# A depthwise convolution beside attention: its columns divided between GpSimd and VectorE, or all on GpSimd

## The chip, the core and the metric

The kernel runs on one NeuronCore of a Trainium2 chip. A core has five engines that run side by side, each working through its own queue in order: TensorE (PE: matrix products; its weight loads are listed as PEld), VectorE (DVE), ScalarE (ACT), GpSimd (POOL) and SyncE (SP, which here only starts transfers). They read and write a common on-chip memory of 128 partitions, and wait for one another at semaphores. The metric is the device time of one execution in microseconds (us); lower is better.

## What is computed

Two layers of a transformer over 1024 latent tokens with a prefix of 256 context tokens, width 1024, all in float32. Each layer normalises and modulates the tokens, projects them to parallel head groups, and adds a mixture of experts behind them. The head groups are attention with 8 query heads and 2 key and value heads of 64 columns, a pooling mixer, and a convolution module, whose 31 taps are the subject here. Cut to what matters:

```python
ql = apply_rope(rms_heads(heads(ql, N_Q_HEADS), q_gain[l]), cos, sin)
attn_l = latent_attention(ql, k_all, v_all)      # softmax over all 1280 keys
yl = jnp.concatenate([attn_l, pool_mixer(ul, ...), conv_module(al, gl, ...)], axis=-1) @ w_out[l]
...
def conv_module(a, g, w_dw, b_dw, cv_g, cv_b, w_pw):
    u = a * jax.nn.sigmoid(g)
    y = lax.conv_general_dilated(u, w_dw[:, None, :], window_strides=(1,),
                                 padding=[(CONV_K // 2, CONV_K // 2)],
                                 dimension_numbers=('NWC', 'WIO', 'NWC'),
                                 feature_group_count=CONV_W) + b_dw
    return jax.nn.silu(ln_affine(y, cv_g, cv_b)) @ w_pw
```

The convolution is depthwise: each of 256 channels has its own 31 weights along the tokens. The first layer computes context and latent tokens, the second only the latent ones (its context tokens give keys and values alone).

## The kernel before

A layer goes through these stages one after the other: a first pass (norms, pooling and convolution inputs), a second pass (queries, keys, values), attention with the convolution beside it, the output projection with routing, and the experts.

**The convolution's data.** Tile A holds the convolution's input with channels on the partitions, 128 channels in each of two halves (f = 0, 1), tokens along the columns; Y receives the result. With the padding between and beside the segments LC is 1340 columns in the first layer and 1054 in the second, so n = LC - 30 is 1310 and 1024 columns of output. A tap (f, k) multiplies a shifted view of A with the channel's weight and adds it to Y; there are 2 x 31 = 62 taps in a layer.

**The division.** CVM = 54 (line 49) says how many of 64 parts of the columns belong to GpSimd: m = 1105 of 1310, and 864 of 1024. `conv_setup` (line 1199) makes two lists. `convq` holds GpSimd's 62 taps; each is two instructions, a product into a scratch region (line 1222) and an addition to Y (line 1223), except the first of each half, which is one (line 1220). `convr` holds VectorE's 62 taps over the other 205 or 160 columns; each is a single instruction (line 1232, the first of each half line 1230) that reads A and Y and writes Y.

**Attention.** `attention` (line 1241) describes its work to a small list scheduler, the class Plan: each operation has an engine, a planned length, what it depends on, and a rank with a name, from which and from the table ATT an order of issue for each engine is fixed when the program is built. The hardware then follows these orders. Pairs of query tiles are taken in turn: in the first layer one short pair (the context's queries, 256 keys), then four full pairs (1280 keys); in the second layer the four full pairs. A pair has 16 steps (8 heads, 2 tiles). A step is: products of queries and keys (PE, lines 1337 and 1338), row maximum (DVE, line 1343, for 1024 and 256 columns apart), its negation (DVE, line 1347), exponential (ACT, line 1355), transposes of the result (PE, line 1360), their copies out of PSUM (DVE line 1367 or ACT line 1369), and products with the values (PE, line 1404). Queries are prepared by lines 1297 to 1313, and each pair's outputs are divided by the sums of the exponentials at lines 1428 to 1446.

**Where the convolution stands in it.** After the queries of the last tile (the list `tail`), the whole of `convq` is one operation of GpSimd (line 1275). Each of `convr`'s taps is an operation of VectorE with the planned length 0.07 + 1.33 * (1 - CVM / 64) = 0.28 us, ranked 3.5 us apart (lines 1276 and 1277). At the end of the plan stand the first steps of the convolution's norm and product (`cpost_steps`): PE transposes two tiles of Y (line 1499). They depend on all of the convolution. Behind attention, `outproj` reads its result (first product at line 1613).

Of the kernel before, what the change touches and what calls it, by code (L numbers as in the profile page):

```python
# [33 lines left out]
# ring of the experts' weights: units of 8 KB per partition, six to an expert; some of them open before the others  # L34
NU, NU0 = 14, 10
# ring of split slices, slices split ahead
# [3 lines left out]
def f32(ap):  # L40
# [7 lines left out]
# of 64 parts of the convolution's columns, those of GpSimd  # L48
CVM = 54
# the attention: microseconds by which operations may come later than their place in the order of the heads  # L50
ATT = {
# [7 lines left out]
class Plan:  # L59
    """operations of several engines with their lengths in microseconds, issued in the order of a list schedule"""  # L60
    LAG = {"DMA": 1.0}

    def __init__(self, prio=None, **slots):
        """slots: numbers of buffers that are taken in turn. prio: by name, the microseconds by which an operation may come later"""
        self.ops, self.slots, self.givers, self.prio = [], slots, {}, prio or {}

    def add(self, eng, length, f, deps=(), rank=(0.0, ""), at=0.0, take=None, give=(), after=None):
        """f issues the operation; eng may be several engines, length and f then lists. A buffer that an operation takes is free
        again after the operations that give it back. rank: microseconds by which it may come later, and its name. after: an
        operation of the same engine that is issued before"""  # L70
        e = [eng] if isinstance(eng, str) else list(eng)
        n = [length] if isinstance(eng, str) else list(length)
        fs = [f] if isinstance(eng, str) else list(f)
        k = len(self.ops)
        self.ops.append((list(zip(e, n, fs)), sorted({d for d in deps if d is not None}), rank, at, take, after))
        for g in give:
            self.givers.setdefault(g, []).append(k)
        return k

    def run(self):  # L80
        """of what can start first, the operation with the longest way to the end goes first"""
# [49 lines left out]
def weave(main, fill):  # L131
    """emit the steps of main in order, those of fill spread among them"""
    j, n, m = 0, len(main), len(fill)
    for i, s in enumerate(main):
        s()
        while j * n < (i + 1) * m:
            fill[j]()
            j += 1
    while j < m:
        fill[j]()  # L140
        j += 1


class Kernel:
# [6 lines left out]
    def later(self, f):  # L151
        """put off a store, so that loads behind it in the queue don't wait for its data"""
        self.stores.append(f)
# [29 lines left out]
    def ln_start(self, src, n=D):  # L183
        """mean and 1 / sqrt(variance + EPS) over n columns"""
# [73 lines left out]
    def mod_load(self, n, pool=None):  # L258
        """start the loads of up to the n-th next step"""
# [9 lines left out]
    def mod_step(self, ahead=1, pool=None):  # L269
# [15 lines left out]
        if k == KD - 1:  # L285
# [5 lines left out]
            if g == 0:  # L291
                # columns to partitions: shift and 1 + scale
# [9 lines left out]
    def layer(self, l):  # L302
# [11 lines left out]
        # blocks of 256 tokens in the order of the passes; the last two of the first pass start the second  # L314
# [42 lines left out]
    # weights of a pass: four units of two k-slices, split in two parts each  # L357
# [36 lines left out]
    def comb_open(self, ctx, l, ny, nx, side="left"):  # L394
        """the tiles that are loaded ahead lie where the last weights but one were; returns a pool that is put below them"""
# [12 lines left out]
    def behind(self, load, i):  # L408
        """a load that lets the scatter of one of the last three experts go first"""
# [17 lines left out]
    def comb0(self, i, t, eng):  # L427
        """gated sum of a token's two experts, times the modulation's gate"""
        self.comb0a(i, t)
        self.comb0b(i, t, eng)  # L430
# [13 lines left out]
    def comb_diag(self, tile_, i):  # L444
        """the gates of a tile's tokens on diagonals"""
# [5 lines left out]
    def comb_pe(self, t, g, ps):  # L451
        """the gated sum by products with diagonals, times the modulation's gate"""
# [12 lines left out]
    def comb2s(self, t):  # L465
        """norm by the vector engine alone, in two steps"""
# [23 lines left out]
    def pass1(self):  # L490
        nc, a, l, last = self.nc, self.a, self.l, self.last
        v, pool = nc.vector, nc.gpsimd
        with ExitStack() as ctx:
# [66 lines left out]
            def th(b):  # L560
                """a block to columns, modulated and split"""
# [138 lines left out]
    def plan1(self, order, sp, below, raws, Wh, Wl, PS, load, where, pb):  # L700
        """first pass of a later layer: combination of the experts' outputs, second residual, norms, products"""
# [18 lines left out]
        # weights of this pass  # L720
# [230 lines left out]
        for n in range(1, nb):  # L951
# [8 lines left out]
            # weights of the second pass  # L960
# [8 lines left out]
    def pass2(self, sp):  # L969
# [3 lines left out]
        with ExitStack() as ctx:  # L973
# [41 lines left out]
            def post(t, part, src=None):  # L1015
                """heads' norms and positions of the queries (part 0), the keys (part 1) or both (part 2), in stages"""
# [183 lines left out]
    def conv_setup(self):  # L1200
# [11 lines left out]
        m = n * CVM // 64  # L1212

        def tap(f, k):
            """the first columns"""
            y, x = self.Y[:, f, 15:15 + m], self.A[:, f, k:k + m]
            t = (self.Y[:, 1, 15:15 + m] if f == 0 else self.A[:, 0, 0:m])
# [7 lines left out]
        def rest(f, k):  # L1225
            """the other columns"""
            y, x = self.Y[:, f, 15 + m:15 + n], self.A[:, f, k + m:k + n]
            w = wdw[:, f, k:k + 1]
            if k == 0:
                nc.vector.tensor_scalar(y, x, w, small[:, 0, f:f + 1], op0=OP.mult, op1=OP.add)  # L1230
            else:
                nc.vector.scalar_tensor_tensor(y, x, w, y, op0=OP.mult, op1=OP.add)  # L1232
        self.convr = [lambda f=f, k=k: rest(f, k) for f in range(2) for k in range(CONV_K)]
# [6 lines left out]
    def attention(self, tail):  # L1240
        nc, l, last = self.nc, self.l, self.last
        with ExitStack() as ctx:
# [19 lines left out]
            def parts(pi):  # L1262
                """columns of the scores: up to 1024 and the rest"""
                n = pairs[pi][1] * 128
                return [(0, min(1024, n))] + ([(1024, n - 1024)] if n > 1024 else [])
# [4 lines left out]
            # the queries of the last tile, then the convolution  # L1270
# [4 lines left out]
            conv = [add(POOL, 4.33 * CONV_K * 2 * CVM / 64, lambda: [c() for c in self.convq], [lastq], (-1000.0, "conv"))]  # L1275
            for k, f in enumerate(self.convr):
                x = add(DVE, 0.07 + 1.33 * (1 - CVM / 64), f, [x], (3.5 * k, "cv"))
            conv.append(x)
# [138 lines left out]
            def norm(pi):  # L1417
                """divide the heads' outputs by the sums of the exponentials"""
# [47 lines left out]
            # the first tiles of the convolution's result  # L1466
# [16 lines left out]
    def cpost_steps(self, sp, pp, q, nm="cps"):  # L1483
        """for a pair of token tiles"""
# [55 lines left out]
    def outproj(self):  # L1540
# [3 lines left out]
        with ExitStack() as ctx:  # L1544
# [61 lines left out]
            def plain(k):  # L1606
                """a slice of the first tile's product, before the weights are split"""
# [53 lines left out]
            def last_res(hf):  # L1661
                """the last tile: first residual and its sums by halves of the columns"""
# [140 lines left out]
    def route_setup(self, wp):  # L1803
# [14 lines left out]
        # per expert: its number + 32 * (assignments in earlier tiles)  # L1818
# [11 lines left out]
    def route(self, ps, t0, t1):  # L1830
        """groups, experts and ranks of the tokens of some tiles; stops after each step"""
# [97 lines left out]
    def pump(self, n=1):  # L1929
        """the next steps of the routing, between other work"""  # L1930
# [9 lines left out]
    def scatters(self, n):  # L1940
        """write the numbers of some assignments to their places"""
# [47 lines left out]
    def route_rows(self, sp):  # L1989
        """where the halves of the products' rows go, counted in half rows: one of the first four chunks of at most 64 tokens  # L1990
        has the second halves of its rows 64 partitions further on"""
# [20 lines left out]
    def moe_open(self):  # L2012
        """buffers for the experts' weights, first loads"""
# [8 lines left out]
    def unit(self, e, j):  # L2022
        """two slices of an expert's weights: four units of gate and up, two of down"""
# [3 lines left out]
    def e_loads(self, lim, q=None):  # L2027
        """start the loads that find room: up to a number of units"""
# [15 lines left out]
    def moe(self):  # L2044
# [3 lines left out]
        with ExitStack() as ctx:  # L2048
# [45 lines left out]
            def prep(e):  # L2094
                """split the tokens and the first slices"""
# [5 lines left out]
            def half(ps, e):  # L2101
                """at most 64 tokens: the two halves of the columns go to two column tiles of the array,
                rows 64 to 127 of the products are the second half"""
# [21 lines left out]
            def full(ps, e, x=None):  # L2125
                """the first half of the columns is ready before the second; then the tokens of a second chunk"""
# [10 lines left out]
            def double(ps, p2, e, m):  # L2137
                """two chunks of tokens; the last place of the slices holds the second one's parts"""
# [45 lines left out]
            def scatter(y, idx, free=True):  # L2184
                """halves of rows to their places"""
# [14 lines left out]
            def one(e, x, ps, g, idx, free, n, lim):  # L2200
                """a whole chunk"""
# [12 lines left out]
            def more(e, n, j, ps, g):  # L2214
                """chunks from the third on"""
# [277 lines left out]
```

## Time and profile before

| | |
|---|---|
| time, median of 3 runs | 3312.55 us (3311.83 to 3315.14) |
| span of the profiled execution, first to last instruction | 3305.2 us |
| its own device time beside the span | not listed apart; the three runs lie 6.6 to 9.9 us above the span |
| PE busy | 2668.3 us (81%) |
| PEld busy | 1678.9 us (51%) |
| DVE busy | 1650.0 us (50%) |
| ACT busy | 1187.4 us (36%) |
| POOL busy | 1006.7 us (30%) |
| mean granted clock of TensorE | 0.906 of full speed |

Busy shares over the whole span mix stages with different limits. The span is better read in slices: the page cuts it into 40 equal ones of 82.6 us and gives each engine's busy share in tenths, and the clock that TensorE was granted in tenths of full speed. Attention fills about 305 to 698 us in the first layer and 1960 to 2307 us in the second.

### The profile page before, as it was taken

What the parts mean: (1) busy time and instruction counts of PE and PEld (TensorE: products, weight loads), DVE (VectorE), ACT (ScalarE), POOL (GpSimd) and SP (SyncE); (2) the same over time, 40 slices, a digit from 0 to 9 for tenths busy, and PEclk for the clock granted to TensorE, in tenths of its full rate; (3) what the DMA queues carried; (4) which work ended last, traced back from release to release, by engine and by line L of the source; (5) the groups of instructions that cost most, each with busy time, mean ns of one, the idle gap of its engine ahead of it and who ended that gap; (6) DMA issues with size and microseconds to landing.
All of it is one profiled execution on the core that took longest, in us unless ns stands there. A gap on an engine that the chain in (4) does not pass through costs nothing. (4 is left out here: it accounts for less than half of the span.)

```text
span 3305.2 us, 41725 instructions
## 1 busy us (share of the span) xinstructions
PE 2668.3 (81%) x13118; PEld 1678.9 (51%) x13118; DVE 1650.0 (50%) x2980; ACT 1187.4 (36%) x2255; POOL 1006.7 (30%) x919
## 2 busy tenths in 40 slices
PE   6987589998678878879756986999967788798884
PEld 4765356667445345446226764565753345454431
DVE  3356975568744323334139669555871233333215
ACT  3223356652134223324125434666311233333212
POOL 1024995013321211211126349900232111111114
PEclk8988789999889989999988998999988899898997
DMA  8541000032487875765986530000359986655895
GB/s 274 202 137 68 1 1 1 1 102 105 182 313 285 302 265 200 258 248 213 365 314 205 170 140 1 1 1 5 143 184 354 348 310 239 228 194 183 318 376 226
DMA packets 280607, 616.66 MB, mean 187 GB/s; under 512 B 63376, under 2 KB 77072, under 8 KB 271504
## 3 DMA queue, kind: packets, MB, share of 16 engines
q1 hardware_dynamic: 251696, 562.24, 46.6%
q0 software_dynamic: 24544, 37.91, 3.3%
q10 hardware_dynamic: 3712, 8.88, 0.7%
q8 instruction: 276, 4.52, 0.6%
q14 instruction: 379, 3.10, 0.3%
HBM read 577.09 MB, written 73.81 MB: 197 GB/s over the span
## 5 line engine op out<-in xcount | busy, mean ns | idle before, releaser
L1343 DVE TENSOR_REDUCE mx<-S 128x1 f32<-128x1024 f32 (+1 forms) x272 | 214.9, 795 | 163.1 <-PE S L1338 163.0
L174 PE MATMUL gu<-wh,xh 128*128 128x512 f32 x432 | 189.8, 439 | 117.2 <-issue 88.4
L1360 PE MATMUL pt<-ident,P 128*128 128x128 f32 x1312 | 221.1, 295 | 78.3 <-ACT P L1355 72.2
L1355 ACT ACTIVATE P<-S,nb 128x256 f32<-128x256 f32 (+1 forms) x272 | 208.6, 773 | 129.5 <-DVE nb L1347 128.1
L2174 PE MATMUL mpy<-er,g 128*128 128x512 f32 (+1 forms) x672 | 243.4, 633 | 8.3 <-issue 8.0
L180 POOL TENSOR_TENSOR rs_out<-ln_ve,mhalf 128x1 f32<-128x1 f32 x64 | 58.7, 918 | 606.2 <-DVE ln_ve L199 372.1
L2188 POOL DMA_INDIRECT y_d<-my,pl x128 | 139.3, 1088 | 315.5 <-ACTq L2280 107.6
L1360 PEld LDWEIGHTS pt<-ident,P 128*128 128x128 f32 x1312 | 152.9, 148 | 158.5 <-ACT P L1355 106.3
L2157 DVE TENSOR_TENSOR sg<-gu,sg 128x256 f32<-128x256 f32 x152 | 57.6, 419 | 351.2 <-ACT sg L2156 351.2
L1404 PE MATMUL po<-PT,V 128*64 128x256 f32 x1312 | 223.3, 419 | 0.3
L1369 ACT ACTIVATE PT<-pt 128x512 f32<-128x512 f32 (+1 forms) x322 | 170.7, 533 | 147.1 <-PE pt L1360 139.2
L2075 PE MATMUL mtp<-ident,xg 128*128 128x128 f32 x600 | 99.9, 298 | 133.1 <-issue 83.4
L2156 ACT ACTIVATE sg<-gu 128x256 f32<-128x256 f32 x152 | 50.3, 383 | 415.9 <-PE gu L2108 258.5
L2187 POOL MEMSET spacer<- 128x1 f32 x152 | 17.6, 116 | 597.7 <-DMA y_d<-my,pl 328.5
L175 PE MATMUL gu<-wl,xh 128*128 128x512 f32 x432 | 183.2, 424 | 9.6 <-DVE wl L170 6.2
L176 PE MATMUL gu<-wh,xl 128*128 128x512 f32 x432 | 182.2, 422 | 4.3 <-issue 4.3
L1337 PE MATMUL S<-KH,Q 128*128 128x512 f32 (+1 forms) x400 | 176.4, 442 | 5.0 <-ACT P L1355 4.6
L170 DVE TENSOR_TENSOR wl<-er,wh 128x1024 fp32r<-128x1024 f32 x102 | 124.3, 1222 | 107.9 <-ACT wh L169 86.4
L2180 DVE COPY my<-mpy 128x512 f32<-128x512 f32 x75 | 51.7, 690 | 251.1 <-PE mpy L2174 243.3
L1232 DVE SCALAR_TENSOR_TENSOR Y<-A,wdw,Y 128x205 f32<-128x205 f32 (+1 forms) x120 | 171.8, 1431 | 1.3
L174 PEld LDWEIGHTS gu<-wh,xh 128*128 128x128 f32 x432 | 89.5, 207 | 162.8 <-issue 138.6
L2108 PE MATMUL gu<-er,xT 128*64 128x512 f32 x720 | 162.1, 594 | 4.6 <-DMA er<-in_w_e_up 1.5
(383 smaller groups left out, 6425.7 us busy)
## 6 DMA issues: line engine op xcount, KB each, us to landing
er<-in_w_e_down SPq DMA_DIRECT2D x66, 1024.0 KB
er<-in_w_e_gate SPq DMA_DIRECT2D x130, 512.0 KB
er<-in_w_e_up SPq DMA_DIRECT2D x130, 512.0 KB
raw<-in_w_mod SPq DMA_DIRECT2D x40, 1024.0 KB
es<-in_w_e_gate SPq DMA_DIRECT2D x64, 512.0 KB
es<-in_w_e_up SPq DMA_DIRECT2D x64, 512.0 KB
es<-in_w_e_down SPq DMA_DIRECT2D x32, 1024.0 KB
raw<-in_w_e_gate SPq DMA_DIRECT2D x40, 512.0 KB
```

Source lines behind the costliest of these rows:

```text
L174: t.matmul(ps, lh, rh, start=start, stop=False)
L175: t.matmul(ps, lh, rl, start=False, stop=False)
L176: t.matmul(ps, ll, rh, start=False, stop=stop)
L1232: nc.vector.scalar_tensor_tensor(y, x, w, y, op0=OP.mult, op1=OP.add)
L1337: tens.matmul(x[:, c:c + w], q, self.KH[:, g, o:o + w], start=True, stop=False)
L1343: v.tensor_reduce(S[st, "mx"][:, ci:ci + 1], S[st, ci][:, 0:cs[ci][1]], axis=AX.X, op=OP.max)
L1355: act.activation(P[st][:, c:c + w], S[st, ci][:, :w], AF.Exp, bias=S[st, "nb"], accum_out=SU[pi][:, i, h, ci:ci + 1])
L1360: tens.transpose(tp[:, j, :], P[st][:, (g_ * 4 + j) * 128:(g_ * 4 + j + 1) * 128], self.ident)
L1369: act.activation(d, TP[st, g_][:, :m, :], AF.Copy)
L1404: tens.matmul(PO[key][o * 64:o * 64 + 64, :], self.V[:, k0(pi) + j, hp // 2, :], PT[pi, 2 * hp + o][:, j, :], start=(j == 0), stop=(j == n ...
L2108: nc.tensor.matmul(ps[0][64 * o:64 * o + 64, :], x[:, k, 0:64], w[:, :, o * 256:(o + 1) * 256], start=(k == 0), stop=(k == KD - 1))
L2174: nc.tensor.matmul(py[o][64 * o:64 * o + 64, :] if hf else py[o], g[:, k % 2, z:z + 64] if hf else g[:, k, :], self.unit(e, 4 + k // 2)[:, ...
```

## The change

The constant CVM goes, and with it the second list: GpSimd's taps cover all n columns, VectorE has none. In the plan the 62 operations of VectorE go, and the planned length of GpSimd's operation is scaled with the layer's columns instead of with CVM. The name "cv" leaves the table ATT. The rest of the diff is comments and line numbers.

```diff
-# of 64 parts of the convolution's columns, those of GpSimd
-CVM = 54
...
         n = self.LC - 30
-        m = n * CVM // 64
 
         def tap(f, k):
-            y, x = self.Y[:, f, 15:15 + m], self.A[:, f, k:k + m]
-            t = (self.Y[:, 1, 15:15 + m] if f == 0 else self.A[:, 0, 0:m])
+            y, x = self.Y[:, f, 15:15 + n], self.A[:, f, k:k + n]
+            t = (self.Y[:, 1, 15:15 + n] if f == 0 else self.A[:, 0, 0:n])
...
-        def rest(f, k):
-            y, x = self.Y[:, f, 15 + m:15 + n], self.A[:, f, k + m:k + n]
-            w = wdw[:, f, k:k + 1]
-            if k == 0:
-                nc.vector.tensor_scalar(y, x, w, small[:, 0, f:f + 1], op0=OP.mult, op1=OP.add)
-            else:
-                nc.vector.scalar_tensor_tensor(y, x, w, y, op0=OP.mult, op1=OP.add)
-        self.convr = [lambda f=f, k=k: rest(f, k) for f in range(2) for k in range(CONV_K)]
...
-            conv = [add(POOL, 4.33 * CONV_K * 2 * CVM / 64, lambda: [c() for c in self.convq], [lastq], (-1000.0, "conv"))]
-            for k, f in enumerate(self.convr):
-                x = add(DVE, 0.07 + 1.33 * (1 - CVM / 64), f, [x], (3.5 * k, "cv"))
-            conv.append(x)
+            conv = [add(POOL, 4.33 * CONV_K * 2 * self.LC / 1310, lambda: [c() for c in self.convq], [lastq], (-1000.0, "conv"))]
```

## Rows read from the trace of the kernel before

**Rows 1.** The page's 40 slices of the span: busy tenths, granted clock.

```profile
DVE  3356975568744323334139669555871233333215
...
PEclk8988789999889989999988998999988899898997
```

**Rows 2.** Windows: stretch, its length, busy us (instructions) of PE, PEld, DVE, ACT, POOL, then PEclk, DMA.

```profile
312.00:448.00 136.00, 84.06 (x357) 53.33 (x355) 132.49 (x149) 47.15 (x115) 129.91 (x71) 0.71 0.00 0
450.00:540.00 90.00, 88.36 (x554) 54.45 (x555) 52.25 (x91) 62.95 (x142) 85.45 (x51) 1.00 0.00 1
...
1969.00:2072.00 103.00, 68.92 (x333) 43.13 (x332) 102.19 (x112) 43.54 (x94) 96.91 (x70) 0.82 0.00 1
```

**Rows 3.** VectorE's groups, 312 to 448 us: count | busy us, mean ns | idle before.

```profile
L1232 DVE SCALAR_TENSOR_TENSOR Y<-A,wdw,Y 128x205 f32<-128x205 f32 x60 | 95.9, 1598 | 0.5
...
L1301 DVE SCALAR_TENSOR_TENSOR q<-qm,q 128x512 fp32r<-128x512 f32 x4 | 4.9, 1237 | 0.0
L1230 DVE TENSOR_SCALAR Y<-A,wdw,cvs 128x205 f32<-128x205 f32 x2 | 4.6, 2304 | 0.0
```

**Rows 4.** VectorE's groups, 1969 to 2073 us.

```profile
L1232 DVE SCALAR_TENSOR_TENSOR Y<-A,wdw,Y 128x160 f32<-128x160 f32 x60 | 75.9, 1265 | 0.8
...
L1230 DVE TENSOR_SCALAR Y<-A,wdw,cvs 128x160 f32<-128x160 f32 x2 | 2.4, 1186 | 0.0
```

**Rows 5.** All instructions of line 1232: ns min/median/max, first and last start.

```profile
L1232 DVE SCALAR_TENSOR_TENSOR Y<-A,wdw,Y x120: 371/1243/2604, 319.3 to 2070.3; 128x205 f32<-128x205 f32 x60, 128x160 f32<-128x160 f32 x60
```

**Rows 6.** Timeline, one tap of each engine: start us, us, engine, line, what.

```profile
355.36 2.52 POOL L1223 TENSOR_TENSOR Y<-Y 128x1105 f32<-128x1105 f32 x1
...
355.81 2.31 DVE L1232 SCALAR_TENSOR_TENSOR Y<-A,wdw,Y 128x205 f32<-128x205 f32 x1
...
357.98 1.19 POOL L1222 TENSOR_SCALAR Y<-A,wdw 128x1105 f32<-128x1105 f32 x1
```

**Rows 7.** Timeline of ScalarE, first layer: exponentials of short, then full steps.

```profile
320.54 0.47 ACT L1355 ACTIVATE P<-S,nb 128x256 f32<-128x256 f32 x1 [1.48 <-DVE nb L1347]
...
327.12 0.47 ACT L1355 ACTIVATE P<-S,nb 128x256 f32<-128x256 f32 x1 [1.56 <-DVE nb L1347]
328.39 0.47 ACT L1355 ACTIVATE P<-S,nb 128x256 f32<-128x256 f32 x1 [0.71 <-DVE nb L1347]
...
362.18 0.47 ACT L1355 ACTIVATE P<-S,nb 128x256 f32<-128x256 f32 x1 [2.55 <-DVE nb L1347]
...
369.59 1.11 ACT L1355 ACTIVATE P<-S,nb 128x1024 f32<-128x1024 f32 x1
...
449.26 1.11 ACT L1355 ACTIVATE P<-S,nb 128x1024 f32<-128x1024 f32 x1 [2.24 <-DVE nb L1347]
...
682.71 1.11 ACT L1355 ACTIVATE P<-S,nb 128x1024 f32<-128x1024 f32 x1 [0.41 <-DVE nb L1347]
```

**Rows 8.** Timeline of ScalarE, second layer: exponentials 1, 15 and 64.

```profile
1974.89 1.11 ACT L1355 ACTIVATE P<-S,nb 128x1024 f32<-128x1024 f32 x1 [2.78 <-DVE nb L1347]
...
2076.74 1.11 ACT L1355 ACTIVATE P<-S,nb 128x1024 f32<-128x1024 f32 x1
...
2291.75 1.11 ACT L1355 ACTIVATE P<-S,nb 128x1024 f32<-128x1024 f32 x1 [0.42 <-DVE nb L1347]
```

**Rows 9.** Timeline of GpSimd: the convolution's first and last instruction, both layers.

```profile
312.11 1.79 POOL L1220 TENSOR_SCALAR Y<-A,wdw,cvs 128x1105 f32<-128x1105 f32 x1
...
538.44 2.14 POOL L1223 TENSOR_TENSOR Y<-Y,A 128x1105 f32<-128x1105 f32 x1
...
1968.76 1.59 POOL L1220 TENSOR_SCALAR Y<-A,wdw,cvs 128x864 f32<-128x864 f32 x1
...
2153.90 2.34 POOL L1223 TENSOR_TENSOR Y<-Y,A 128x864 f32<-128x864 f32 x1
```

**Rows 10.** Timeline of PE: first transpose of the convolution's result, both layers.

```profile
684.53 0.44 PE L1499 MATMUL pt<-ident,Y 128*128 128x128 f32 x2
...
2295.71 0.38 PE L1499 MATMUL pt<-ident,Y 128*128 128x128 f32 x2
```

2 rows, old and new, of the table ATT are left out of this document.

## The prediction, made before the changed kernel was run

> **What bounds the kernel now.** I read the page's slices first. VectorE's digits stand at 9 in the 5th slice (330 to 413 us) and the 25th (1983 to 2066 us), where attention begins in each layer, and TensorE's clock digits there are 7 and 8 [rows 1]. The windows then say why. From 312 to 448 us VectorE is busy 132.5 of 136 us while TensorE has 84 of 136 at a mean clock of 0.71; from 450 to 540 us VectorE is busy only 52 of 90 us, and TensorE 88 of 90 at full clock [rows 2]. So attention has two regimes: a front part limited by VectorE, and a rest limited by TensorE. The second layer shows the same front part, 102.2 of 103 us [rows 2].
>
> VectorE's groups name the load: the convolution's 62 instructions take 95.9 + 4.6 = 100.5 us of the first front part [rows 3] and 75.9 + 2.4 = 78.3 us of the second [rows 4]. The plan counts 0.28 us for each; they take 1.6 and 1.26 us on average. The shortest takes 371 ns and the longest 2604 [rows 5], for shapes that differ by only 205 to 160 columns, so most of it is not arithmetic. One pair of taps shows what it is: VectorE's instruction starts at 355.81, while GpSimd's addition has run since 355.36, and ends at 358.12, just after GpSimd's addition has ended (357.88) and its next product has begun [rows 6]. VectorE is held for as long as GpSimd's addition lasts, and the maxima and negations behind it in its queue are late; the exponentials wait for "nb", the negated maximum, in most rows of the front part [rows 7].
>
> **The change part by part.** *VectorE's taps go.* 178.8 us of VectorE's busy time go in two layers. That is not the gain: TensorE is next. What the front part takes without them I read step by step.
>
> Short steps, first layer: 16 exponentials from 320.54 to 362.18, 15 intervals in 41.6 us [rows 7], 2.78 us each. Where no long tap fell between, two followed each other in 1.27 us [rows 7], so 15 x 1.27 = 19.1 us and a gain of 22.6. Ends: 1.0 us each (about two exponentials of 0.47), a gain of 26; or 1.8, half way to today's, a gain of 15. I take 1.27, since it is measured with the same dependencies.
>
> The turn to full steps, 362.18 to 369.59 [rows 7], I leave at its 7.4 us: it is made of query preparation and the short pair's division, which stay.
>
> Full steps, first layer: the first to the tenth exponential take 449.26 - 369.59 = 79.7 us, 8.85 each; the tenth to the 64th take 682.71 - 449.26 = 233.5 us for 54 intervals, 4.32 each, limited by TensorE [rows 7]. Nine at 4.32 make 38.9: gain 40.8. Second layer: exponentials 1 to 15 take 101.9 us, 15 to 64 take 215.0 for 49 intervals, 4.39 each [rows 8]. Fourteen at 4.39 make 61.4: gain 40.4.
>
> Ahead of the first exponential one tap of line 1230 goes, 2.3 and 1.2 us on average [rows 3, 4]; part of that hides behind query preparation, and I count 1 us in each layer, 0 to 2.
>
> Sum: 22.6 + 40.8 + 40.4 + 2 = 105.8 us.
>
> *GpSimd's taps get longer.* It runs from 312.11 to 540.58, 228.5 us, and from 1968.76 to 2156.24, 187.5 us [rows 9]. Scaled by the columns, 1310/1105 and 1024/864, it is 270.9 and 222.2 us, ending at 583.0 and 2191.0. That is an upper bound as far as the arithmetic goes, since a fixed part of an instruction does not grow, and since the taps no longer meet VectorE's. Nothing else waits for it before the transposes of line 1499. TensorE reaches these at 684.53 and 2295.71 [rows 10]; brought forward by 65 and 42 us, at 619 and 2254. So 36 and 63 us of slack remain, and I cost the longer taps at nothing. If that cover went, line 1499 would stand in TensorE's queue, and behind it the last products of attention, for which the output projection waits.
>
> *GpSimd in the way of VectorE's other work.* The query preparation of line 1301, which reads two on-chip tensors as the taps did, averages 1.24 us in the front part [rows 3], and there are few such instructions. From 450 to 540 us GpSimd convolves all the time, 85.5 of 90 us, and TensorE is still full [rows 2]. So this contention remains and costs nothing that the 4.32 does not already hold.
>
> *A price from the notes.* The Trainium skill, GPSIMD Engine Reference, section Key points, says that for elementwise work VectorE is structurally about twice as fast as GpSimd, which speaks against this change. By columns the trace agrees at best: 205 columns on GpSimd cost about 3.7 x 205/1105 = 0.7 us a tap (228.5 us over 62 taps is 3.7 [rows 9]), and VectorE's shortest tap takes 0.37 [rows 5]. By that rule the sum would be a loss, 271 + 222 - 228.5 - 187.5 = 77 us of GpSimd for at most 62 x 2 x 0.28 = 35 us of VectorE; by the rows it is not, since VectorE's taps average 1.4 us and GpSimd has slack.
>
> *The plan is made anew.* Its 62 operations of VectorE go, and the convolution's planned length changes from 226.5 to 274.6 and 216.0 us. Orders may shift. The nearest rows are the two layers' orders, 4.32 against 4.39 a step [rows 7, 8]: 0.07 x 128 steps = 9 us either way. I take 0.
>
> The profiled span is 3305.2 us and the median 3312.55, 7.35 above; the change touches nothing outside the span, so I take the gain off the median: 3312.55 - 105.8 = 3206.7, say **3206 us**.
>
> **The rivals.** *TensorE stays at half clock in the front part.* It has a mean of 0.71 of full speed there, between 1.2 and 2.4 GHz, with 52 of 136 us idle [rows 2]. If half of the 23 full intervals went at twice 4.35 us, 11.5 x 4.35 = 50 us of the gain would go: 3256. For it: the short pair leaves gaps in TensorE's work. Against: as soon as VectorE lets go, the clock is 1.00 [rows 2].
>
> *GpSimd becomes the bound, and the kernel gets slower.* Place: line 1499 in the first layer, where TensorE waits for the last tap. It eats gain once a tap takes over (619 - 312)/62 = 4.95 us and makes that layer slower over (684.5 - 312)/62 = 6.0; I expect at most 270.9/62 = 4.4. At 6.5 us a tap the first layer ends 31 us later than now, and the second, at 5.2, gains 5: 3339. The durations of the same instructions at two lengths (1105 and 864 columns) run nearly in proportion, 3.7 and 3.0 us a tap [rows 9], which speaks against a jump at 1310. The skill's rule above points to this rival, but it holds no threshold.
>
> *The wait only changes hands.* VectorE is in the front part late for another reason, say a copy or maximum that waits for TensorE, and the freed time turns into idle time: no difference, 3312. Against it: VectorE is busy 97% there, with idle time of 0.5 us before the taps [rows 2, 3].
>
> *More than forecast.* The first steps of a layer have no products with values to do yet, so that they could run below 4.32 us. At 3.3 for five steps in each layer, 10 us more; with the short steps at 1.0, 14 us: 3192.
>
> **How the numbers follow.** Forecast 0.78, with a range of its own from 3185 (14 more, plan 7 better) to 3225 (short steps 8 less, the plan 9 worse, start 2 less). More than that, 0.05. Half clock for a part of the steps 0.11, reaching up to 3256. Changes hands 0.03. GpSimd the bound 0.03. The range that holds 8 in 10 goes from 3180 to 3240. 0.2%, 6.6 us, is about what a measurement of this kernel can tell from no change. Faster by more: 0.78 + 0.05 + 0.11 = 0.94; within 0.03; slower 0.03.
>
> **What would show it.** In the changed profile, VectorE's busy share at the start of both attentions should fall from near 100% to some 55%, TensorE's clock there rise to near 1, exponentials follow each other in about 4.3 us from the second or third full step on, and in 1.3 us in the short pair. GpSimd's convolution should last about 260 to 271 and 213 to 222 us, and line 1499 should start at about 619 and 100 us or so earlier in the second layer (42 plus the first layer's 65), without a wait for GpSimd. The prediction is wrong if TensorE stands idle for "nb" or for GpSimd in these parts, or if full steps at the front stay above 5 us.

## The result, and the profile after

The changed kernel takes 3210.07 us (median of 4 runs, 3205.37 to 3218.59) against 3312.19 us before, a gain of 102.1 us. The ratio is 0.9701, with a 95% interval of 0.9679 to 0.9723. The forecast was 3206, with a range of 3180 to 3240.

The profiled execution has a span of 3211.5 us, 93.7 below the 3305.2 of before. That is less than the medians' gain because of the executions that were profiled: the one of the changed kernel took 3213.33 us, 3.3 above its median, and its time is 1.8 us above its span; at the same distance the one of before stands about 5 us below the median of the timed four. The page's slices, as in [rows 1]; a slice is now 80.3 us:

```profile
DVE  3355556487543323334149555556851332333215
...
PEclk8998999999799889999878999999978899899997
```

VectorE's 9 of the two attention starts is gone (its digits stand at 5 there), and TensorE's clock digit there is 9.

The windows of the same places as in [rows 2] (stretch, its length, busy us of PE, PEld, DVE, ACT, POOL with counts, then PEclk):

```profile
312.00:345.00 33.00, 24.77 (x140) 18.10 (x140) 22.52 (x51) 20.52 (x60) 31.91 (x16) 0.86 0.00 1
345.00:450.00 105.00, 101.22 (x616) 63.94 (x615) 57.38 (x100) 72.99 (x164) 100.82 (x47) 0.97 0.00 1
1913.00:1978.00 65.00, 58.38 (x349) 38.58 (x349) 33.81 (x55) 45.48 (x99) 61.64 (x40) 0.93 0.00 1
```

From 312 to 450 us, the first two windows together, VectorE is busy 79.9 of 138 us and TensorE 126.0; before, from 312 to 448 us, it was the other way round, 132.5 and 84.1 of 136 [rows 2]. GpSimd is as busy as it was, 132.7 of 138 us against 129.9 of 136.

The exponentials in ScalarE's timeline, which answer to [rows 7] (first layer: first and last short step, full steps 1, 10 and 64) and [rows 8] (second layer: 1, 15 and 64). They are now on line 1339:

```profile
320.12 0.47 ACT L1339 ACTIVATE P<-S,nb 128x256 f32<-128x256 f32 x1
...
337.15 0.47 ACT L1339 ACTIVATE P<-S,nb 128x256 f32<-128x256 f32 x1
...
344.89 1.11 ACT L1339 ACTIVATE P<-S,nb 128x1024 f32<-128x1024 f32 x1 [2.50 <-DVE nb L1331]
...
384.33 1.12 ACT L1339 ACTIVATE P<-S,nb 128x1024 f32<-128x1024 f32 x1
...
620.34 1.11 ACT L1339 ACTIVATE P<-S,nb 128x1024 f32<-128x1024 f32 x1 [0.41 <-DVE nb L1331]
...
1920.71 1.11 ACT L1339 ACTIVATE P<-S,nb 128x1024 f32<-128x1024 f32 x1
...
1978.51 1.11 ACT L1339 ACTIVATE P<-S,nb 128x1024 f32<-128x1024 f32 x1
...
2193.37 1.12 ACT L1339 ACTIVATE P<-S,nb 128x1024 f32<-128x1024 f32 x1 [0.42 <-DVE nb L1331]
```

Read against the rows of before they give a table by step, in us. "Start" is the first query preparation of attention, "end" the output projection's first product (lines 1297 and 1613 before, 1281 and 1597 after). Before, these stood at 305.67 and 698.49, and at 1962.33 and 2307.38; after, at 306.54 and 642.48, and at 1907.07 and 2209.14.

| step | before | forecast | after |
|---|---|---|---|
| layer 1: start to first exponential | 14.9 | 13.9 | 13.6 |
| 15 intervals of short steps | 41.6 | 19.1 | 17.0 |
| turn to full steps | 7.4 | 7.4 | 7.7 |
| full steps 1 to 10 | 79.7 | 38.9 | 39.4 |
| full steps 10 to 64 | 233.5 | 233.5 | 236.0 |
| last exponential to end | 15.8 | 15.8 | 22.1 |
| layer 2: start to first exponential | 12.6 | 11.6 | 13.6 |
| full steps 1 to 15 | 101.9 | 61.4 | 57.8 |
| full steps 15 to 64 | 215.0 | 215.0 | 214.9 |
| last exponential to end | 15.6 | 15.6 | 15.8 |

The first layer's attention is 56.9 us shorter and the second's 43.0, together 99.9. All other stages of this one execution are 6.2 us longer, which gives the 93.7 of the span; 4.5 of them lie behind the second layer's attention, where the code is the same. The four runs of the changed kernel differ by up to 13.2 us.

GpSimd's convolution, first and last instruction of each layer, as in [rows 9], and the transposes that wait for it, as in [rows 10]:

```profile
312.97 1.97 POOL L1216 TENSOR_SCALAR Y<-A,wdw,cvs 128x1310 f32<-128x1310 f32 x1
...
574.41 2.50 POOL L1219 TENSOR_TENSOR Y<-Y,A 128x1310 f32<-128x1310 f32 x1
...
1913.50 1.72 POOL L1216 TENSOR_SCALAR Y<-A,wdw,cvs 128x1024 f32<-128x1024 f32 x1
...
2125.93 2.38 POOL L1219 TENSOR_TENSOR Y<-Y,A 128x1024 f32<-128x1024 f32 x1
```

```profile
631.90 0.44 PE L1483 MATMUL pt<-ident,Y 128*128 128x128 f32 x2
...
2195.19 0.44 PE L1483 MATMUL pt<-ident,Y 128*128 128x128 f32 x2
```

It lasts 263.9 and 214.8 us (before 228.5 and 187.5) and ends at 576.9 and 2128.3, 55 and 67 us before TensorE asks for it.

What went wrong in the first layer's tail stands in TensorE's waits from 629 to 645 us (engine, line, what it waited for: us, times, longest):

```profile
PE pt L1496 <- ACT cyn L1491: 1.8, 1, 1.8
PE pt L1507 <- ACT A L1500: 1.8, 1, 1.8
PE py L1597 <- ACT Y L1511: 0.7, 1, 0.7
```

Before, these steps of the convolution's norm were strewn among the last products of attention, from 684.5 on. Now they all stand behind them, and TensorE goes through transposes, ScalarE's activations and the pointwise product in turn, with nothing else to do. These waits make 4.3 us. The products between them are also slower: from 634 to 642.5 us TensorE was granted 0.60 of full speed, near the lower of its two levels (1.2 of 2.4 GHz), after it had been at 1.00 and nearly always busy up to 632 us. The pointwise product, first in the changed kernel and then in E1 (below), where the clock was 1.00:

```profile
638.01 3.78 PE L1507 MATMUL pt<-A,wpw 128*128 128x256 f32 x8 [1.78 <-ACT A L1500]
```

```profile
633.65 2.00 PE L1507 MATMUL pt<-A,wpw 128*128 128x256 f32 x8
```

### The profile page after: what moved, and what is told of

It is laid out like the page before. It is cut to its first block, busy times and chain, and to the rows that moved or that the text cites. A ratio compares the mean times of both kernels' runs of the same rounds, so it can differ in the third digit from the quotient of the medians.

```text
span 3211.5 us, 41598 instructions
## 1 busy us (share of the span) xinstructions
PE 2635.0 (82%) x13118; PEld 1663.1 (52%) x13118; DVE 1493.3 (46%) x2851; ACT 1188.0 (37%) x2260; POOL 1070.6 (33%) x919
## 5 line engine op out<-in xcount | busy, mean ns | idle before, releaser
L1344 PE MATMUL pt<-ident,P 128*128 128x128 f32 x1312 | 206.7, 282 | 10.1 <-ACT P L1339 10.0
L1388 PE MATMUL po<-PT,V 128*64 128x256 f32 x1312 | 212.5, 403 | 0.1
L1344 PEld LDWEIGHTS pt<-ident,P 128*128 128x128 f32 x1312 | 145.3, 141 | 83.4 <-ACT P L1339 41.5
L1321 PE MATMUL S<-KH,Q 128*128 128x512 f32 (+1 forms) x400 | 168.8, 423 | 1.5 <-ACT P L1339 1.5
L2059 PEld LDWEIGHTS mtp<-ident,xg 128*128 128x128 f32 x600 | 77.8, 155 | 173.8 <-issue 125.2
```

What stands on the lines that cost most here:

```text
L1321: tens.matmul(x[:, c:c + w], q, self.KH[:, g, o:o + w], start=True, stop=False)
L1344: tens.transpose(tp[:, j, :], P[st][:, (g_ * 4 + j) * 128:(g_ * 4 + j + 1) * 128], self.ident)
L1388: tens.matmul(PO[key][o * 64:o * 64 + 64, :], self.V[:, k0(pi) + j, hp // 2, :], PT[pi, 2 * hp + o][:, j, :], start=(j == 0), stop=(j == n ...
L2059: nc.tensor.transpose(tp[:, j, :], x[:, k * 128:(k + 1) * 128], self.ident)
```

## The experiments

Attention's length below is always from "start" to "end" as in the table: 392.8 and 345.1 us before, 335.9 and 302.1 after.

**E1: the plan's length for GpSimd, alone.** In the changed kernel:

```diff
-            conv = [add(POOL, 4.33 * CONV_K * 2 * self.LC / 1310, lambda: ...
+            conv = [add(POOL, 4.33 * CONV_K * 2 * 54 / 64, lambda: ...
```

> The changed kernel, but the plan counts GpSimd's convolution at 226.5 us in both layers, as the plan of before did, in place of 274.6 and 216.0. This alone brings the first steps of the convolution's norm back among the last products of attention in TensorE's order. Theory (the tail is an effect of the plan): from the last exponential to the output projection's first product the first layer takes 15.8 us as before the change, not 22.1, and the median falls by 6 to 8 us to about 3203. Rival (the tail waits for GpSimd's longer convolution, or for something else): the tail stays at about 22 us and the median at about 3210.

Measured: 3203.36 us (3200.52 to 3207.86), ratio 0.9677 (0.9664 to 0.9691). The transposes and the projection's first product in TensorE's timeline, first layer:

```profile
624.68 0.44 PE L1483 MATMUL pt<-ident,Y 128*128 128x128 f32 x2
628.64 0.44 PE L1483 MATMUL pt<-ident,Y 128*128 128x128 f32 x2
638.64 3.70 PE L1597 MATMUL py<-raw,qm 128*128 128x512 f32 x8 [0.58 <-DVE qm L1430]
```

From the last exponential (622.86) to the projection it is 15.8 us again, attention takes 329.3 and 302.0. TensorE's order agrees: between "start" and the first transpose the first layer's trace has 1830 of its instructions, as before the change, and 1890 in the changed kernel. The intervals of the two ratios overlap, so that the 6.7 us between the medians rest on the 6.4 us of the tail in the profiles. With E9, which cannot be told from it, this is the fastest kernel that computes everything.

**E2: VectorE's taps left out.** The kernel before without 60 of VectorE's 62 taps; the other columns hold only the first tap's product.

```diff
-        self.convr = [lambda f=f, k=k: rest(f, k) for f in range(2) for k in range(CONV_K)]
+        self.convr = [lambda f=f, k=k: rest(f, k) for f in range(2) for k in range(1)]
```

> The kernel before with 60 of VectorE's 62 taps of a layer left out (the first of each half stays, so the other columns hold only the first tap's product); GpSimd keeps its 54 of 64 parts. Theory (VectorE's taps alone slowed the front): the front part vanishes as in the changed kernel, first full steps at about 4.3 us, from the convolution's start to the output projection's first product about 322 us in the first layer and 295 in the second, median about 3203. Rival (the gain came from GpSimd's single list or the new order of issue): some part of the front stays, the median lies above 3230.

Measured: 3210.74 us (3200.34 to 3215.82), attention 329.6 and 303.3 us, from the first query preparation to the projection's first product:

```profile
302.20 1.13 ACT L1297 ACTIVATE q<-qm 128x512 fp32r<-128x512 f32 x2
...
631.81 1.55 PE L1613 MATMUL py<-raw,qm 128*128 128x512 f32 x3 [0.58 <-DVE qm L1446]
...
1900.47 1.13 ACT L1297 ACTIVATE q<-qm 128x512 fp32r<-128x512 f32 x2
...
2203.73 2.08 PE L1613 MATMUL py<-raw,qm 128*128 128x512 f32 x2 [0.58 <-DVE qm L1446]
```

The lengths that were expected count from the convolution's start, and so counted these are 323.2 and 296.8. With GpSimd's part untouched, removing VectorE's taps gives all of the gain. Output values change here and in E3, and with them the routing of tokens to experts, so that attention's length says more than the total.

**E3: GpSimd's taps left out, VectorE's kept.** The same edit on the loop that fills `convq`.

```diff
         for f in range(2):
-            for k in range(CONV_K):
+            for k in range(1):
                 steps.append(lambda f=f, k=k: tap(f, k))
```

> The kernel before with 60 of GpSimd's 62 taps of a layer left out (the first of each half stays); VectorE's 62 taps, their columns and their places are as before. Theory (a tap of VectorE is held while GpSimd's addition runs): VectorE's taps take 0.37 to 0.45 us for 205 columns in place of 1.60 and less for 160, the front part ends, and the median is 3200 to 3215, although VectorE does all its taps. Rival (a tap with two on-chip inputs costs VectorE 1.3 to 1.6 us by itself): the taps stay above 1.2 us and the median near 3310.

Measured: 3184.87 us (3173.55 to 3189.97), attention 322.3 and 297.7 us. VectorE's groups in the first layer's attention, which answer to [rows 3]:

```profile
L1232 DVE SCALAR_TENSOR_TENSOR Y<-A,wdw,Y 128x205 f32<-128x205 f32 x60 | 25.8, 429 | 0.5
L1230 DVE TENSOR_SCALAR Y<-A,wdw,cvs 128x205 f32<-128x205 f32 x2 | 1.6, 776 | 0.0
```

The same 60 instructions on the same columns take 25.8 us in place of 95.9. A tap of 205 columns is 0.43 us of VectorE's own work; the other 1.17 of the 1.60 was waiting inside the instruction for GpSimd. The rival, that the taps are dear by themselves, is out. The median lies 15 us below the lower end of the range: attention became shorter even than in the changed kernel, by 18 us. Of these 6.4 are the first layer's tail, which is 15.8 us here as in E1; against E1, attention is 11.3 us shorter. VectorE's other instructions are no longer held either, which fits: query preparation (line 1301) lasts 0.69 us at most in E3, in the changed kernel up to 2.44. How much of the 11.3 us is that was not separated.

**E4: all columns on VectorE.** CVM = 0, and GpSimd's operation is left out of the plan.

```diff
-CVM = 54
+CVM = 0
...
-            conv = [add(POOL, 4.33 * CONV_K * 2 * CVM / 64, ...)]
+            conv = []
```

> The kernel before with CVM = 0: all columns on VectorE, GpSimd has no taps. The opposite division. Theory (held by GpSimd, else VectorE's taps cost their columns): with GpSimd silent a tap of 1310 columns takes about 1.45 us, less than the 1.60 that 205 columns took beside GpSimd; 62 of them are 90 us, about what VectorE spent before, but spread over the whole of attention by the plan, where VectorE has some 40% idle; the median lies between 3200 and 3235. Rival (a fixed cost of 1.2 us or more a tap, columns on top): 2.5 us a tap, 155 us a layer, VectorE becomes the bound of attention and the median is 3300 or more.

Measured: 3266.01 us (3260.98 to 3276.61), ratio 0.9877, attention 364.2 and 337.3. VectorE's group in the first layer's attention:

```profile
L1232 DVE SCALAR_TENSOR_TENSOR Y<-A,wdw,Y 128x1310 f32<-128x1310 f32 x60 | 94.7, 1578 | 0.2
```

The tap's price is as expected (1.58 us): all 1310 columns cost VectorE 94.7 us, about as much as 205 did beside GpSimd. The time is not: 31 us more than the upper end. The first explanation was that the plan puts taps into every gap, so that they are done by 470 us, with VectorE 84 to 93% busy until 450.

**E5: the same, spread.**

```diff
-                x = add(DVE, 0.07 + 1.33 * (1 - CVM / 64), f, [x], (3.5 * k, "cv"))
+                x = add(DVE, 0.07 + 1.33 * (1 - CVM / 64), f, [x], (3.5 * k, "cv"), 8.0 + 4.2 * k)
```

> All columns on VectorE again, but the plan lets tap k start no earlier than 8.0 + 4.2 k us into attention; before, the plan put taps into every gap, and they were done after half of attention. Theory (the loss against the changed kernel is bunching: taps of 1.6 us in a VectorE that is 85 to 90% busy delay the maxima): with about one tap a step, steps stay at 4.3 to 4.5 us, attention takes 322 to 335 us in the first layer and 298 to 310 in the second, the median is 3190 to 3215. Rival (a long tap in front of a maximum costs its time wherever it stands): attention stays near 364 and 337 us, the median near 3266.

Measured: 3272.37 us (3261.94 to 3277.43), attention 368.4 and 339.0. That is 57 us above the range and near the rival's numbers: bunching was not the reason. In the first layer full steps 15 to 64 now take 243.3 us, with 41 taps among them and VectorE busy only about 70%; before, without a tap there, they took 215.2. TensorE's waits from 450 to 620 us:

```profile
PE pt L1360 <- ACT P L1355: 15.8, 9, 3.3
PE pt L1306 <- DVE q L1301: 2.7, 1, 2.7
```

Most of them are for exponentials, as in the front part of before. So a tap costs attention 0.6 to 0.7 us (28.1 us over 41 taps; 28.6 over 47 in the second layer) although VectorE has idle time on the whole. Whether it is the tap in front of the maximum, or the PSUM copies that the plan then gives to ScalarE (192 of the 208 in the first layer's attention, 166 in the changed kernel), was not separated.

**E6: VectorE's taps after GpSimd's, division as before.**

```diff
+            x = conv[0]
             for k, f in enumerate(self.convr):
                 x = add(DVE, 0.07 + 1.33 * (1 - CVM / 64), f, [x], (3.5 * k, "cv"))
```

> The kernel before, its division kept, with VectorE's taps ordered behind GpSimd's part in the plan, so that they run when GpSimd has finished or nearly. Theory (held by GpSimd): taps take 0.33 to 0.45 us, 62 of them 23 us in VectorE's idle time, the front part vanishes, but the norm's first steps now stand at the very end as in the changed kernel, in both layers: attention some 336 and 308 us, median 3210 to 3225. Rival (own cost of 1.3 us or more a tap): 80 us of taps in the last 65 us of attention, the end of attention is 20 to 30 us late in each layer, median 3250 or more.

Measured: 3246.50 us (3234.63 to 3251.19), ratio 0.9809, attention 346.1 and 328.7. VectorE's group at the end of the first layer's attention:

```profile
L1232 DVE SCALAR_TENSOR_TENSOR Y<-A,wdw,Y 128x205 f32<-128x205 f32 x60 | 25.8, 430 | 1.3
```

The taps cost 0.43 us, as in E3, with everything computed, and the front is as fast as in the changed kernel (full steps 1 to 10 in 39.5 us). The time is 21 us above the upper end, for the place: the taps start at 600 us, though GpSimd is done at 542, and VectorE's steps of the norm come behind all of them, so that the tails are 26.8 and 41.4 us. The theory of the taps holds, that of the place in the plan was too optimistic.

**E7: half as many columns for VectorE.** CVM = 59: 103 and 80 columns.

> The kernel before with CVM = 59: VectorE has 103 columns of 1310 in place of 205 (80 of 1024 in place of 160), GpSimd the rest. Theory (a tap is held as long as GpSimd's running instruction, whatever its own length): taps still take 1.4 to 1.7 us in the first layer, the front part stays, median 3290 to 3330. Rival (the price goes by VectorE's columns): taps take half, about 0.8 us, the front part shrinks by half, median about 3260.

Measured: 3342.62 us (3340.0 to 3346.55), ratio 1.0107 (1.0085 to 1.0130): 1.1% slower than before, with fewer columns for VectorE, and 13 us above the upper end of the range. Its groups in the two front parts:

```profile
L1232 DVE SCALAR_TENSOR_TENSOR Y<-A,wdw,Y 128x103 f32<-128x103 f32 x60 | 105.5, 1759 | 0.6
```

```profile
L1232 DVE SCALAR_TENSOR_TENSOR Y<-A,wdw,Y 128x80 f32<-128x80 f32 x60 | 74.5, 1241 | 1.0
```

A tap of 103 columns takes 1.76 us and one of 205 took 1.60 [rows 3]; one of 80 takes 1.24 and one of 160 took 1.26 [rows 4]. The price does not go by VectorE's own columns, and that rival is out. In the first layer it rose by 10% where GpSimd's columns rose by 9% (1207 for 1105), in the second it did not rise.

Held taps explain only part of the slowdown. Attention is 33.1 us longer, while VectorE's taps take 10.7 us more in the first layer and no more in the second. The planned lengths changed too (0.17 us a tap), and with them the order: 29 taps instead of 22 stand among the short steps, which are 15.9 us longer. And in the second layer the norm's first steps now stand behind attention's last products, as in the changed kernel's first layer, and its tail is 6.5 us longer.

**E8: the division of before, spread** (the edit of E5 with CVM = 54).

> The kernel before, its division kept (54 of 64), with VectorE's taps spread over attention as in e5: tap k no earlier than 8.0 + 4.2 k us. Theory (held taps cost what exceeds VectorE's idle time): those taps that run beside GpSimd still take 1.3 to 1.7 us, but one a step finds room; most of the front part vanishes, attention some 340 to 355 us and 305 to 320, median 3215 to 3245. Rival (a held tap delays the step that it stands in by its own time): the front part is only drawn out, 54 taps of 1.5 us, attention above 375 us in the first layer, median near 3300.

Measured: 3244.78 us (3234.69 to 3255.66), ratio 0.9819, attention 347.0 and 325.1. Within the range, at its upper end; the second layer is 5 us beyond. VectorE's group beside GpSimd, in the first layer:

```profile
L1232 DVE SCALAR_TENSOR_TENSOR Y<-A,wdw,Y 128x205 f32<-128x205 f32 x36 | 40.4, 1122 | 0.0
```

The 36 taps average 1.12 us, less than the 1.3 to 1.7 expected; the last 20 run after GpSimd is done and take 0.42. So spreading alone gives 63% of what E2 gains in the two attention stretches (65.8 of 105.0 us). It both sets the taps apart and leaves less of them beside GpSimd, and what each of these gives was not separated. Of the 34 us to the changed kernel's attention, 11.0 lie in the second layer's full steps 15 to 64, 7.6 in its tail (23.4 us), some 12 in the two fronts and 3.6 in the first layer's full steps 10 to 64.

**E9: another small instruction that is held.** E1, with the sum of two partial sums of 8 columns written as a reduction:

```diff
-                            v.tensor_tensor(x, SU[pi][:, i, :, 0], SU[pi][:, i, :, 1], op=OP.add)
+                            v.tensor_reduce(x, SU[pi][:, i, :, :], axis=AX.X, op=OP.add)
```

> The kernel of e1, with one small thing more: each pair's sums of exponentials are put together by a reduction over the last axis (one on-chip input) in place of an addition of two on-chip tensors. Theory (VectorE is held beside GpSimd only where its instruction reads two on-chip tensors or takes a mode that uses the same access, as the additions of 8 columns that last up to 2.45 us in the changed kernel and at most 0.16 where GpSimd is silent): the reductions last about 0.15 us throughout, the 16 instructions save some 6 us of VectorE, and the median falls by 0 to 6 us to 3197 to 3203. Rival (any instruction of VectorE that reads the common memory is held): the reductions last up to 2.4 us like the additions, the median stays at 3203.

Measured: 3202.69 us (3192.75 to 3207.11), ratio 0.9678 (0.9652 to 0.9704); attention 326.3 and 300.4 us, against 329.3 and 302.0 in E1. All instructions of the line, ns min/median/max, in the changed kernel and then in E9:

```profile
L1412 DVE TENSOR_TENSOR ri<-sums x16: 114/158/2448, 410.3 to 2196.7; 128x8 f32<-128x8 f32 x16
```

```profile
L1412 DVE TENSOR_REDUCE ri<-sums x16: 117/136/160, 410.7 to 2186.4; 128x8 f32<-128x16 f32 x16
```

An addition of 8 columns lasts up to 2.45 us beside GpSimd; of the reductions, which read the same numbers as one tensor, none lasts over 0.16 us. The total cannot be told from E1's.

## Why the prediction was right

*The bound and the mechanism.* Right. VectorE limited the front of attention, since its taps were held while GpSimd's instructions ran. The prediction read this from one pair of rows [rows 6]; E3 and E6 show it: the same taps cost 0.43 us with GpSimd silent or finished. E7 shows that their price beside GpSimd does not go by their own columns. The Trainium skill, SBUF — State Buffer, section Who interferes with whom, says it as a rule: an instruction of VectorE with two on-chip inputs contends with one of GpSimd that reads the memory, the later one is fully blocked, and on this chip a reduction never contends. The pair of [rows 6] agrees with the first part: the tap that started second ends 0.24 us after GpSimd's addition (alone it takes 0.43, so that not quite all of it was blocked). E9's two rows agree with the last: 2448 ns at most for the addition, 160 for the reduction.

*What the freed time is worth.* Right in size. Of 178.8 us of VectorE's time the prediction counted 105.8, because TensorE is next; the medians moved by 102.1. By terms: the short steps gained 24.6 for 22.6 forecast, the first layer's full steps 40.2 for 40.8, the second's 44.1 for 40.4. The start gained 1.3 in the first layer and lost 1.1 in the second, for 1 each.

Two of the terms came out larger. The 1.27 us of a short step was read where no long tap fell between, but one of 0.96 us did, at 327.28; without any the steps follow in 17.0 / 15 = 1.14 us. And the first full steps run below the 4.32 us, as "more than forecast" said: the second layer's first product with values starts at 1937.4, with the fifth full step, and intervals 2 to 5 take 3.6 us each. In the first layer intervals 2 to 5 take 3.5, but the first one takes 7.8, so that its term did not grow.

That the sum fits so well is in part luck. The terms that came out larger make some 6 us and what came out smaller some 12 (the tail 6.4, the first layer's steps 10 to 64 2.6, the starts 1.8, the turn 0.3, its first full steps 0.6), so that attention gained 99.9 us for 105.8. That the medians' 102.1 is nearer to it is a difference from run to run.

Some of its smaller sums are off, and none of it matters for the time: the first layer's terms make 64.4 us and not 65, the value half way from 1.27 to today's 2.78 is 2.0 and not 1.8, and of the 7.35 us between median and span only about 2 are the program's own, the rest being another execution.

*GpSimd's longer part costs nothing.* Right for what waits for it: 263.9 and 214.8 us, below the bounds of 270.9 and 222.2, done 55 us ahead of the transposes. The rival that ended slower had its threshold at 4.95 us a tap; a tap took 4.26. That GpSimd in VectorE's way costs nothing beyond the 4.32 us of a step was not tested by itself; E3, whose attention is 11.3 us shorter than E1's in both layers together, bounds it.

*The plan made anew.* This is the term that was mis-sized: 0 taken, 9 either way as bound. The new planned length moved the norm's first steps to the end of TensorE's order and cost 6.4 us in the first layer, as E1 shows, and the first layer's full steps 10 to 64 took 2.6 more. Together this just fills the bound, and the bound came from the wrong place: it was taken from the pitch of a step, while most of the loss sits in the tail, which the prediction left as it was without naming it. Why those steps took longer was not tested; in E1 they take 235.8 us, 2.3 more than before.

*Half clock.* Did not happen in the front: 0.86 from 312 to 345 us, 0.97 from 345 to 450 and 0.93 at the start of the second layer. It did in the first layer's tail, where the prediction had not looked (0.60).

*The price from the Trainium skill.* The factor of about two that the prediction cites (GPSIMD Engine Reference, Key points) is a ratio of 2.7 for a tap here: 1310 columns take 1.58 us on VectorE (E4) and 4.26 on GpSimd, in two instructions. To choose by it would have been wrong here: E4, with all columns on VectorE, is 56 us slower than the changed kernel. VectorE's work lies ahead of attention's maxima, while what waits for GpSimd has 55 us to spare; which part of E4's loss is the taps themselves and which the copies that moved to ScalarE stays open (E5).

## What to carry to other kernels

Before dividing elementwise work between VectorE and GpSimd, look at the shortest and the mean duration of VectorE's instructions of one shape: 0.42 beside 1.60 us for 205 columns was the sign here that they wait inside, and a smaller share for VectorE made nothing better (E7). What mattered was who stands on the chain: GpSimd took 2.7 times as long for the work, but nothing waited for it. And where a scheduler's planned length changes, look for what it puts at the end of each queue (6.4 us in the first layer's tail, E1).

## What was not expected of the hardware

That fewer columns for VectorE made the kernel slower (E7, ratio 1.0107) was not foreseen in sign: the forecast of that run had no change as its middle. Part of it is the plan's new order, as said there.

GpSimd's additions of equal length differ by their operands. In the changed kernel's groups of the first layer (1310 columns) and the second (1024):

```profile
L1219 POOL TENSOR_TENSOR Y<-Y 128x1310 f32<-128x1310 f32 x30 | 90.2, 3007 | 2.5
L1219 POOL TENSOR_TENSOR Y<-Y,A 128x1310 f32<-128x1310 f32 x30 | 75.9, 2528 | 2.5
```

```profile
L1219 POOL TENSOR_TENSOR Y<-Y,A 128x1024 f32<-128x1024 f32 x30 | 71.5, 2382 | 2.5
L1219 POOL TENSOR_TENSOR Y<-Y 128x1024 f32<-128x1024 f32 x30 | 61.1, 2037 | 2.5
```

In the first layer the addition with scratch in Y is the slower one by 19%, in the second the one with scratch in A by 17%: 1.9 to 2.0 against 2.3 ns a column. E1 and E9 have the same durations within 2%. Since the same tiles change places between the layers, it may hang on where the two operands lie; no run tried that.
